# Accumulating transfers moved from one stage to another, and an order between GpSimd's additions and VectorE's two-operand operations

## The chip, the cores and the metric

The kernel runs on one core of one Trainium2 chip. The core has five engines that run side by side and wait for one another through semaphores: TensorE (PE in the profile: matmuls, with weight loads listed as PEld), VectorE (DVE), ScalarE (ACT), GpSimd (POOL) and SyncE (SP), which issues most of the DMA transfers. The metric is the device time of one execution in microseconds (us), the median of several runs. It was 2028.37 us before the change (three runs, 2027.73 to 2028.91).

## What is computed

Two layers of a decoder trunk on a sequence of 1024 tokens with 1024 channels, in float32. A layer has a mixer block (latent attention, a gated convolution, causal pooling, window attention, side by side) and a feed-forward block, each with a residual add:

```python
for l in range(DEPTH):
    h = rmsnorm(x, attn_norm[l])
    proj = h @ w_in[l]
    ...
    x = x + mixed @ w_o[l]
    h2 = rmsnorm(x, ffn_norm[l])
    gate, up = jnp.split(h2 @ w_gate_up[l], 2, axis=-1)
    x = x + (jax.nn.silu(gate) * up) @ w_down[l]
return rmsnorm(x, final_norm)
```

The feed-forward block has 2816 hidden channels, 22 tiles of 128.

## The kernel before

**Staging.** Activations are kept with channels on the 128 partitions and tokens along the free dimension, in two halves of 512 tokens. Each float32 matrix product is made of three matmuls: every operand is split into a high part in a rounded format (a cast on ScalarE, L368) and a low part (original minus high, a subtraction on VectorE, L371), and high x high, high x low and low x high are summed in PSUM (`mm3`, L348). So every weight tile passes through ScalarE and VectorE before TensorE can use it. The order of the stages, for each of the two layers, is: projections and mixers, output projection, gate/up (L1727 and after), down projection.

**Gate/up.** The gate/up and down products use a scheme with seven block products in place of eight, which needs sums of weight blocks. A step handles one f of the 22 hidden tiles: seven products of twelve matmuls (B11, B21, N2, N1, T3, B22, T4). Step 0 is done plainly. For steps 3 to 21 GpSimd makes the sums: three additions in `GateUp.sums` (L1330 to L1332) and one in `sum4` (L1360), each 128x512, for the step that follows. For steps 1 and 2 there is no time for that at the stage's start. Their sums lie ready in DRAM (`made`, buffers gd), built earlier by accumulating DMA transfers that GpSimd issues: a plain transfer writes a weight block into gd, and transfers with an add put further blocks on top. `gu_made(l)` (L306) is a generator that issues one of six such transfers for each of the two tiles at every call of `next`, twelve a layer. Each is held (`paced`, L297) until the matmul that was traced last before it has run, and one on the same bytes waits for the one before it. The sums are read at L1324, L1354 and L1365.

**Who calls the generator.** `project()` (L540) multiplies by one tile of the input weights for both halves; a layer has twelve such calls. Each begins with two calls of `next(sums, None)`, so a layer's twelve transfers go out during its own first six projections. `dn_made` yields nothing here, because `DN_MADE` is empty.

**GpSimd's other work.** In gate/up it also multiplies the SiLU by the norm factor (`silu`, L1570 on ScalarE, then L1572 on GpSimd; VectorE's L1564 takes the result) and makes sums of down weights in quarters (`dn_sum`, L1650, loaded by L1643, stored by L1653). In the mixers it clears parts of score tiles (L1158). On VectorE, L1450, L1776 and L1788 add PSUM results to copies, L449 multiplies, and `combos` (L1581, L1583) combines activations.

**The order of the work.** The program is traced, and then the class `Order` plans it: it simulates the five queues with a cost for each instruction, ranks instructions by when their results are due, improves the order with random trials, and picks the best of its plans by trials with drawn delays. The planned order of each queue is then imposed (`impose`): instructions of one queue follow one another as planned, without any semaphore. In this simulation a VectorE operation whose operands all lie in SBUF (kind "two": tensor by tensor, tensor by scalar, copy) and an addition on GpSimd (kind "pool") hold one port in turn: each waits for the other's end, less 0.14. `passing` gives the time that a transfer takes on the DMA engines, `costs` its time to landing, and `LATE` is added to loads.

Of the kernel before, what the change touches and what calls it, by code (L numbers as in the profile page):

```python
# [20 lines left out]
P = 128  # L21
D = 1024
S = 1024
L = 2
# [102 lines left out]
def trunk_kernel(ctx: ExitStack, tc: tile.TileContext, ins, out, given=None, ends=None):  # L127
# [212 lines left out]
    sums = iter(())  # L340
# [177 lines left out]
    for l in range(L):  # L518
        if l == 0:
            expect_layer(0)  # L520
        sums = chain(gu_made(l), dn_made(l))


        def proj(w, t, tag="mm"):
# [13 lines left out]
            return p  # L538

        def project():  # L540
            next(sums, None)
            next(sums, None)
            w = take()
            pp = [proj(w, t) for t in range(2)]
            ahead()
            return pp
# [399 lines left out]
        for t in range(2):  # L946
            s = F.half()
# [580 lines left out]


        acts = {f: [None, None] for f in range(3)}  # L1530

        def plain(u):

# [200 lines left out]
        for f in range(3, NFF):  # L1734
# [2 lines left out]
            wnn = GateUp(f + 2) if f + 2 < NFF else None  # L1737
            end = f == NFF - 1
            gu_start(w, lambda: pending and second(*pending))
            if f % 2:  # L1740
                g = f // 2
                sp.dma_start(ad_of(B11, g), F.ap(acts[2 * g][HALVES.index(0)]))
# [192 lines left out]
class Order:  # L1935
# [54 lines left out]

    @classmethod
    def passing(cls, i):
        return cls.size(i.outs[0]) * P * 4 / 400e3 if i.opcode == "DMACopy" else 0.0

    @classmethod
    def wide(cls, i):
# [17 lines left out]
    def costs(cls, i):  # L2014
# [5 lines left out]
        if op == "DMACopy":  # L2020
            t = cls.passing(i)
            if e == "Pool":
                return 1.5 * t + 3.5, 0.9
            if cls.kinds(i) == "load":
                return t + (1.85 if t < 0.7 else 2.1), 0.34
            return t + 1.35, 0.34
# [37 lines left out]
    def run(self, rank, back=False, fixed=None, draw=None):  # L2064
# [16 lines left out]
        order = {e: [] for e in self.ENGINES}  # L2081
        flying, served = deque(), 0.0
        port = {"two": 0.0, "pool": 0.0}
        other = {"two": "pool", "pool": "two"}
        for k in range(self.n):
            if not left[k]:
# [8 lines left out]
        while todo:  # L2095
# [34 lines left out]
            seen, taken = cost[k]  # L2130
            if draw:
                late = 2.5 * draw.random() if draw.random() < 0.25 else 0.0
                if e in ("DVE", "Activation", "Pool"):
                    more = draw.gauss(0.0, 0.02) * seen
                    seen, taken = seen + more, taken + more
            order[e].append(k)
            if back:
                free[e] = t + taken * (self.SHARED if kind[k] == "pool" else 1.0)
                end[k] = -free[e]
            else:  # L2140
                if kind[k] in port:
                    more = max(0.0, port[other[kind[k]]] - t - self.LEAST)
                    seen, taken = seen + more, taken + more
                    port[kind[k]] = t + seen
                free[e], end[k] = t + taken, t + seen
                if self.moved[k]:
                    if kind[k] == "load":
                        end[k] += late
                    served = end[k] = max(end[k], served + self.moved[k])
                if e == "SP":  # L2150
                    flying.append(end[k])
                    if len(flying) > self.LANES:
                        flying.popleft()
            for j, sync in ahead[k]:
# [9 lines left out]
                if not left[j] and fixed is None:  # L2164
                    heapq.heappush(later[self.engine[j]], (ready[j], j))
        return end, order

    def trial(self, order):

# [86 lines left out]
def scheduled_kernel(fresh, ins_of, rounds=1):  # L2256

    def trace(banks, ends, order=None):  # L2260
        nc = fresh()
        ins, out = ins_of(nc)
        with tile.TileContext(nc) as tc:
# [4 lines left out]
                if Order.queue(i) in Order.ENGINES and i.opcode != "TilePoolBoundary"  # L2268
            ]
            if order is not None:  # L2270
                Order.impose(tc, traced, order)
        return nc, traced, asked

    nc, traced, asked = trace(None, None)
# [1 line left out]
    for slow in SLOW:  # L2276
        plan, asked, first.slow = first, tried, slow
        end = plan.find()[2]
        for _ in range(rounds):
# [3 lines left out]
            best = plan.find()  # L2283
            end = best[2]
            order = plan.improve(best, 30)[1]
            found.append((plan.trial(order), given, order))
    best = min(found, key=lambda x: x[0])
    return trace(*best[1], best[2])[0]


def _constants():
# [132 lines left out]
```

## Time and profile before

| what | value |
|---|---|
| median of three runs | 2028.37 us |
| the profiled execution, its own time | 2028.42 us |
| its span, first to last instruction | 2026.6 us |
| granted TensorE clock, mean | 0.999 |
| DMA, share of 16 engines for SyncE's queue | 47.0% |
| DMA, share for GpSimd's queue | 3.3% |
| mean DMA rate | 167 GB/s |

The profile page starts with each engine's busy time. A row of a group reads: line of the kernel, engine, operation, tiles written and read, shape and count, then busy us and mean ns of one, then the idle time of that engine just ahead of these instructions and what ended it. Waits read: who waited, for whom, us in total, how often, the longest. A timeline row reads: start, length, engine, line, operation, and in brackets the idle time ahead of it and what released it. TensorE's matmuls overlap one another, and their ends are modelled, so its busy time says that it had work, not that it ran at full pitch. The stages can be told from the windows: in layer 0 mixers run to about 400 us, gate/up to about 800, the down projection to about 1000; layer 1 follows about 1003 us later.

### The profile page before, as it was taken

The page shows a single profiled execution, that of the slowest core. Times are in us where ns is not written, and L with a number is a line of the kernel's source. Part 1 is how long each engine was busy: PE and PEld are TensorE (multiplying, and loading weights), DVE is VectorE, ACT ScalarE, POOL GpSimd, SP SyncE. Part 2 cuts the span into 40 slices and gives each one's busy share as a digit, 9 for nine tenths or more (in the row PEclk, how much of TensorE's full clock was granted, in tenths as well). Part 3 has the DMA queues.
Part 4 walks back from the last instruction along what each step waited for, and adds up shares of the span by engine and source line. Part 5 has one row for each costly group of instructions (what it writes and reads, how often), then busy time and mean ns, then how long its engine had stood idle before and what let it go on. Part 6 is the DMA issues. An engine that isn't in the chain of part 4 may idle for free.

```text
span 2026.6 us, 26712 instructions
## 1 busy us (share of the span) xinstructions
PE 2015.0 (99%) x9418; PEld 1679.6 (83%) x9418; DVE 1521.4 (75%) x2330; ACT 1023.4 (50%) x1770; POOL 570.3 (28%) x428
## 2 busy tenths in 40 slices
PE   9999999999999999999999999999999999999998
PEld 8888888888888888888888888888888888888887
DVE  8789988997666668776646898789976766785554
ACT  8457657743333335555533676678333333354343
POOL 0100000057776772000001000000687677710000
PEclk9999999999999999999999999999999999999999
DMA  6531223345545547998835234242554554487552
GB/s 207 110 63 45 75 101 112 113 141 195 178 163 198 178 162 268 378 352 294 278 97 131 63 94 137 81 136 102 174 172 167 201 172 168 163 312 254 184 179 84
DMA packets 154231, 338.56 MB, mean 167 GB/s; under 512 B 14960, under 2 KB 62192, under 8 KB 154096
## 3 DMA queue, kind: packets, MB, share of 16 engines
q1 hardware_dynamic: 149616, 325.31, 47.0%
q0 software_dynamic: 4480, 11.54, 3.3%
q8 instruction: 74, 1.21, 0.3%
q14 instruction: 61, 0.50, 0.1%
HBM read 241.36 MB, written 105.91 MB: 171 GB/s over the span
## 4 chain that ended last, share of the span: by engine, by line
PE 98%; ACT 1%; DVE 0%; DMA 0%; issue 0%; DVEq 0%; ACTq 0%
PE ps_mm L348 38%; PE ps_s L348 30%; PE ps_t L348 12%; PE ps_pv L348 8%; PE ps_pv L1161 2%; PE ps_t L1149 2%; PE ps_s L1091 1%; PE ps_s L1092 1%; PE ps_s L1093 1%; PE ps_s L962 1%; PE ps_pv L763 1%; PE ps_s L685 1%; PE ps_t L428 1%; PE ps_t L751 1%; DMA u<-in_w_gu 0%; ACT u L368 0%
## 5 line engine op out<-in xcount | busy, mean ns | idle before, releaser
L348 PE MATMUL ps_mm<-u,u 128*128 128x512 f32 (+1 forms) x3378 | 825.4, 388 | 1.0 <-DVE tm L449 0.9
L348 PEld LDWEIGHTS ps_mm<-u,u 128*128 128x128 f32 x3378 | 616.8, 188 | 120.7 <-DVE tm L449 1.3
L371 DVE TENSOR_TENSOR u<-u,u 128x1024 fp32r<-128x1024 f32 (+3 forms) x461 | 508.7, 1124 | 182.0 <-ACT u L368 159.7
L348 PE MATMUL ps_s<-u,u 128*128 128x512 f32 x2670 | 634.1, 389 | 0.1
L348 PEld LDWEIGHTS ps_s<-u,u 128*128 128x128 f32 x2670 | 501.2, 188 | 104.7 <-DVE u L1298 0.5
L368 ACT CAST u<-u 128x1024 fp32r<-128x1024 f32 (+3 forms) x461 | 389.4, 864 | 376.4 <-DMA u<-ad 68.6
L348 PE MATMUL ps_t<-u,u 128*128 128x512 f32 (+1 forms) x1124 | 253.5, 377 | 0.1
L1572 POOL TENSOR_TENSOR tm<-tm,u 128x512 f32<-128x512 f32 x80 | 141.1, 1764 | 341.5 <-ACT tm L1570 335.7
L348 PEld LDWEIGHTS ps_t<-u,u 128*128 128x128 f32 x1124 | 202.5, 188 | 39.4 <-DVE u L1379 0.5
L348 PE MATMUL ps_pv<-u,u 128*128 128x512 f32 x744 | 177.4, 389 | 0.0
L348 PEld LDWEIGHTS ps_pv<-u,u 128*128 128x128 f32 x744 | 139.6, 188 | 29.0
L322 POOL DMA_DIRECT2D gd<-in_w_gu x24 | 21.3, 888 | 413.1 <-PE ps_t L348 280.7
L1158 POOL MEMSET u<- 128x128 f32 x32 | 5.9, 210 | 427.0 <-PE ps_mm L348 191.7
L1570 ACT ACTIVATE tm<-tm 128x512 f32<-128x512 f32 x80 | 50.6, 632 | 133.2 <-DVE tm L449 133.2
L1438 ACT COPY tm<-ps_s 128x512 f32<-128x512 f32 x61 | 35.8, 588 | 107.2 <-PE ps_s L348 107.1
L368 ACT CAST u<-ps_t 128x512 fp32r<-128x512 f32 (+3 forms) x132 | 64.3, 503 | 48.7 <-PE ps_t L1149 26.4
L371 DVE TENSOR_TENSOR u<-ps_t,u 128x512 fp32r<-128x512 f32 (+3 forms) x132 | 74.8, 582 | 16.0 <-ACT u L368 14.8
L1650 POOL TENSOR_TENSOR u<-u,u 128x352 f32<-128x352 f32 x64 | 80.0, 1251 | 1.4
L1360 POOL TENSOR_TENSOR u<-u 128x512 f32<-128x512 f32 x38 | 68.1, 1793 | 39.7 <-DVE u L371 39.7
L373 ACT ACTIVATE u<-u,par 128x512 fp32r<-128x512 f32 x99 | 69.7, 716 | 18.0 <-DVE u L1298 8.5
L412 ACT ACTIVATE tm<-u 128x512 f32<-128x512 f32 (+1 forms) x91 | 53.9, 599 | 47.2 <-DVE u L1841 39.6
L374 DVE SCALAR_TENSOR_TENSOR u<-u,par,u 128x512 fp32r<-128x512 f32 x99 | 72.3, 745 | 6.1 <-ACT u L373 5.6
(205 smaller groups left out, 2296.6 us busy)
## 6 DMA issues: line engine op xcount, KB each, us to landing
u<-in_w_gu SPq DMA_DIRECT2D x84, 512.0 KB, 4.1
ad<-u SPq DMA_DIRECT2D x154, 256.0 KB, 3.2
u<-ad SPq DMA_DIRECT2D x70, 512.0 KB, 5.8
u<-in_w_dn SPq DMA_DIRECT2D x64, 352.0 KB, 3.3
qd<-u SPq DMA_DIRECT2D x64, 352.0 KB, 2.6
u<-in_w_in SPq DMA_DIRECT2D x43, 512.0 KB, 4.8
u<-qd SPq DMA_DIRECT2D x32, 512.0 KB, 5.3
u<-in_w_dn SPq DMA_DIRECT2D x24, 512.0 KB, 5.4
```

The source lines that it names most:

```text
L348: last_mm = pe.matmul(o, w, r, start=start and k == 0 and i == 0, stop=stop and k == n - 1 and i == 2, skip_group_check=again,)
L368: a = act.copy(hi, f)
L371: dve.tensor_tensor(out=lo, in0=f, in1=rd(hi), op=ALU.subtract)
L373: a = act.activation(hi, f, AF.Copy, scale=gain)
L374: dve.scalar_tensor_tensor(out=lo, in0=f, scalar=gain, in1=rd(hi), op0=ALU.mult, op1=ALU.subtract)
L412: act.activation(q, f, AF.Square)
L1149: pe.transpose(p[:, b * P : (b + 1) * P], pr[b][j // 4][:, (j % 4) * P : (j % 4 + 1) * P], ident,)
L1161: pe.matmul(py[:, c0:], v_of(j, h), R.ap(s)[:, c0:], start=j == 0 and n == 0, stop=j == nj - 1 and n == 1,)
L1360: pool.tensor_tensor(out=q4, in0=q4, in1=F.ap(self.raw[1] + 1), op=ALU.add)
L1570: last_silu = act.activation(g, g, AF.Silu)
L1572: pool.tensor_tensor(out=g, in0=g, in1=r, op=ALU.mult)
L1650: pool.tensor_tensor(out=o, in0=a, in1=b, op=ALU.add)
```

## The change

The change has four parts.

1. Layer 1's twelve accumulating transfers leave layer 1's projections. A generator `made_next = gu_made(l + 1)` is made in layer 0, and each gate/up step from 3 on takes one transfer from it, just after `gu_start`. Layer 1's `project` finds nothing to issue.
2. Layer 0's transfers go one, not two, to a projection.
3. The planner's figures for GpSimd's transfers change: 2.5 times the passing time on the DMA engines, other constants to landing, loads twice as late while such a transfer is under way, and larger drawn delays then.
4. `Order.turns` walks through the planned order and pairs an addition on GpSimd with the last VectorE operation of kind "two" that ends before it starts, if one has ended since the pair before. `impose` adds a dependency with a semaphore for each pair: the addition then waits for that operation.

```diff
-        sums = chain(gu_made(l), dn_made(l))
+        sums = chain(gu_made(l) if l == 0 else (), dn_made(l))
...
         def project():
             next(sums, None)
-            next(sums, None)
             w = take()
...
         acts = {f: [None, None] for f in range(3)}
+        made_next = gu_made(l + 1) if l + 1 < L else iter(())
...
             gu_start(w, lambda: pending and second(*pending))
+            if l + 1 < L:
+                next(made_next, None)
             if f % 2:
...
     def passing(cls, i):
-        return cls.size(i.outs[0]) * P * 4 / 400e3 if i.opcode == "DMACopy" else 0.0
+        if i.opcode != "DMACopy":
+            return 0.0
+        t = cls.size(i.outs[0]) * P * 4 / 400e3
+        return t * (2.5 if cls.queue(i) == "Pool" else 1.0)
...
             if e == "Pool":
-                return 1.5 * t + 3.5, 0.9
+                return 1.2 * t + 3.0, 0.9
...
+        summed = 0.0
...
                 late = 2.5 * draw.random() if draw.random() < 0.25 else 0.0
+                if t < summed:
+                    late += 4.0 * draw.random() if draw.random() < 0.4 else 0.0
...
                     if kind[k] == "load":
                         end[k] += late
+                        if t < summed and not draw and fixed is None:
+                            end[k] += late
+                    elif e == "Pool":
+                        summed = end[k]
...
+    def turns(self, order):
+
+        end, _ = self.run(None, fixed=order)
+        start = [x - s for x, (s, _) in zip(end, self.cost)]
+        two = [k for k in order["DVE"] if self.kind[k] == "two"]
+        pairs, i = [], 0
+        for g in order["Pool"]:
+            if self.kind[g] != "pool":
+                continue
+            d = None
+            while i < len(two) and end[two[i]] <= start[g] + self.LEAST:
+                d = two[i]
+                i += 1
+            if d is not None:
+                pairs.append((d, g))
+        return pairs
...
-    def impose(tc, traced, order):
+    def impose(tc, traced, order, turns):
+        for a, b in turns:
+            tc.add_manual_dep(
+                traced[b],
+                traced[a].name,
+                mybir.DependencyInfo(mybir.DependencyClass.Sync, mybir.DependencyReason.DATA),
+                reason="turn",
+            )
```

The rest of the diff hands `turns` from the planner to `impose`.

More of the change, by code (lines that the diff above doesn't have):

```diff
@@ L2256, in scheduled_kernel, with trace @@
 def scheduled_kernel(fresh, ins_of, rounds=1):
-    def trace(banks, ends, order=None):
+    def trace(banks, ends, order=None, turns=()):
         nc = fresh()
@@ L2270, in trace @@
             if order is not None:
-                Order.impose(tc, traced, order)
+                Order.impose(tc, traced, order, turns)
         return nc, traced, asked
@@ L2285, in scheduled_kernel @@
             order = plan.improve(best, 30)[1]
-            found.append((plan.trial(order), given, order))
+            found.append((plan.trial(order), given, order, plan.turns(order)))
     best = min(found, key=lambda x: x[0])
-    return trace(*best[1], best[2])[0]
+    return trace(*best[1], *best[2:])[0]
 def _constants():
```

## The prediction

> **What bounds the kernel now.** I read the page first: the busy shares, then the chain that ended last, then the waits of TensorE (PE), and last the stages by windows.
>
> ```profile
> PE 2015.0 (99%) x9418; PEld 1679.6 (83%) x9418; DVE 1521.4 (75%) x2330; ACT 1023.4 (50%) x1770; POOL 570.3 (28%) x428
> PE 98%; ACT 1%; DVE 0%; DMA 0%; issue 0%; DVEq 0%; ACTq 0%
> PE ps_pv L579 <- DVE ones_r L198: 1.3, 1, 1.3
> PE ps_mm L348 <- DVE tm L449: 0.9, 1, 0.9
> PE ps_s L435 <- ACT tm L434: 0.5, 1, 0.5
> ```
>
> The second line is the chain by engine; the last three are all of TensorE's waits in the span: 2.7 us. Span minus busy time is 2026.6 - 2015.0 = 11.6 us, and most of it lies at the two ends, as the chain in order of time shows:
>
> ```profile
> 1.32 4.65 PE ps_pv L579 x20
> 93.21 21.79 PE ps_mm L348 x96
> 41.95 3.68 PE ps_mm L348 x16
> 2017.46 0.71 PE ps_s L435 x2
> ```
>
> The first matmul starts at 1.3 us and the last ends at 2018.2, so 8.4 us follow it; 11.6 - 1.3 - 8.4 leaves 1.9 us of visible idle time between. Busy time hides short bubbles, because the matmuls overlap, so I count matmuls by stage. Columns of the next view: stretch, its length, PE, PEld, DVE, ACT, POOL busy with counts, clock, DMA share, GB/s.
>
> ```profile
> 50.00:400.00 350.00, 349.02 (x1744) 292.38 (x1744) 309.31 (x648) 225.88 (x490) 13.28 (x27) 1.00 0.32 90
> 450.00:750.00 300.00, 300.00 (x1325) 248.39 (x1325) 204.73 (x209) 103.88 (x142) 223.01 (x158) 1.00 0.54 182
> 1050.00:1400.00 350.00, 349.93 (x1746) 292.64 (x1745) 289.95 (x624) 221.51 (x482) 12.75 (x27) 1.00 0.37 108
> 1450.00:1750.00 300.00, 300.00 (x1325) 248.43 (x1324) 209.44 (x211) 104.75 (x144) 220.61 (x156) 1.00 0.53 182
> ```
>
> In gate/up (rows 2 and 4) 300/1325 = 0.2264 us a matmul, the same number in both layers: full pitch, nothing to win there. In the mixers (rows 1 and 3) the chain's pieces run from 21.79/96 = 0.2270 to 3.68/16 = 0.2300 us, so bubbles hide between 0.0006 and 0.0036 us in each of 1744 + 1746 matmuls: an estimate of 2 to 13 us in all, in pieces far under 0.1 us. The granted clock is 1.00. So TensorE sets the time, and the change can shorten only what those bubbles and the 1.9 us hold.
>
> **The change part by part.**
>
> *Twelve transfers leave layer 1's projections; layer 0's twelve go one, not two, to a projection.* The accumulating transfers (L322) build the weight sums of gate/up steps 1 and 2 in DRAM.
>
> ```profile
> L322 POOL DMA_DIRECT2D gd<-in_w_gu x24: 551/846/1172, 40.9 to 1120.5; - x24
> L1324 SPq DMA_DIRECT2D u<-gd x4: 382/536/1466, 346.0 to 1351.8; - x4
>   POOL gd L322: 75.3, 13
>   ACT u L368: 5.5, 3
> DMA to landing us min/median/max: 3.1/5.3/10.5
> 117.02 0.85 POOL L322 DMA_DIRECT2D gd<-in_w_gu  x1 [6.90 <-DVE sm L694]
> gd<-in_w_gu POOLq DMA_DIRECT2D x20, 512.0 KB, 6.5
> 40.00:130.00 90.00, 90.00 (x458) 76.03 (x457) 71.47 (x168) 37.79 (x95) 10.69 (x12) 1.00 0.49 96
> u<-in_w_in SPq DMA_DIRECT2D x4, 512.0 KB, 3.5
> 213.98 0.35 POOL L1158 MEMSET u<- 128x128 f32 x2 [96.11 <-PE ps_mm L348]
> ```
>
> Rows three and four name all who waited for such a transfer or its result: the next of its kind on GpSimd, and ScalarE 5.5 us. TensorE is not among them. A weight load (in_w_in) lands after a median 3.5 us both in 40 to 125 us, where layer 0's twelve run, and in 125 to 230, where none does. So taking them out of layer 1 frees nothing TensorE waits for: 0 us. In layer 0 twelve projections now carry one each. The last was issued at 117 us; the twelfth projection is traced just ahead of the code that clears the first score tile, at 214, so I estimate the last issue near there. The sums are first read at 346: some 130 us stay, against a landing of at most 10.5. What it is moved past on GpSimd's queue is the clearing of score tiles (L1158), first at 214 us after 96 us of idle time: one issue (0.85 us) and at worst one landing ahead of it. 0 us.
>
> *The twelve go to layer 0's gate/up, one a step.* A step is seven products of twelve matmuls, 84 x 0.2264 = 19.0 us. GpSimd is busy 223.01/300 of it, 14.1 us, so 4.9 are idle. One issue of 0.85 us makes it 15.0 of 19.0. The predecessor it must wait for was issued 19 us earlier and lands in 10.5 at most, and its other wait, for a TensorE matmul just traced, is placed by the plan. Queued behind it are the sums for the next step (L1330 to L1332, L1360), the down-projection sums (L1650) and the product of the SiLU (L1572); for these wait ScalarE's split and VectorE's L1564. Cost 0 while the 4.9 us hold. On the DMA side each adds 512 KB to a stage at a share of 0.54, and the landings above show no queueing at 0.49 where they ran before: 0 us, at worst some tenths for a load that lands late.
>
> [...]
>
> *GpSimd's additions wait for VectorE's two-operand operations.* The plan pairs an addition with the last such operation that ends before it and adds a semaphore wait. Now the trace has both engines holding each other up:
>
> ```profile
> 397.23 1.30 POOL L1572 TENSOR_TENSOR tm<-tm,u 128x512 f32<-128x512 f32 x1 [63.37 <-ACT tm L1570]
> 415.26 6.83 POOL L1572 TENSOR_TENSOR tm<-tm,u 128x512 f32<-128x512 f32 x1 [16.73 <-ACT tm L1570]
> 415.56 4.16 DVE L371 TENSOR_TENSOR u<-u,u 128x512 fp32r<-128x512 f32 x5
> 811.61 1.21 DVE L371 TENSOR_TENSOR u<-u,u 128x1024 fp32r<-128x1024 f32 x1
> 589.70 0.69 DVE L449 TENSOR_TENSOR tm<-tm,u 128x512 f32<-128x512 f32 x1
> 589.80 1.39 POOL L1650 TENSOR_TENSOR u<-u,u 128x352 f32<-128x352 f32 x1
> 590.32 1.97 DVE L371 TENSOR_TENSOR u<-u,u 128x1024 fp32r<-128x1024 f32 x1
> ```
>
> An addition alone takes 1.30 us; behind an unbroken run of VectorE operations it took 6.83. VectorE's long split takes 1.21 us alone, 1.97 with an addition between. So they exclude each other, and the wait mostly renames time already lost. Where it isn't neutral is the last three rows: the addition was already standing at 589.80 when L449 ended at 590.39, and got in ahead of the split that was issued at 590.32. Told to wait for L449's end, it comes after the split: GpSimd loses one slot of 1.21 us, VectorE gains it.
>
> Is a slot covered? VectorE reaches TensorE's results ahead of time, which is the margin (450 to 750 us):
>
> ```profile
> POOL tm L1572 <- ACT tm L1570: 55.8, 20, 6.1
> POOL u L1360 <- DVE u L371: 17.1, 13, 2.7
> DVE tm L1788 <- PE ps_mm L348: 13.2, 7, 2.0
> DVE tm L1776 <- PE ps_s L348: 10.6, 6, 2.6
> DVE u L1564 <- POOL tm L1572: 7.1, 10, 1.2
> ```
>
> Its waits for products average 13.2/7 = 1.9 and 10.6/6 = 1.8 us, while TensorE waits for none. A delay of GpSimd that reaches VectorE through L1564 or a split uses up this margin first, and GpSimd's own waits for ScalarE (55.8 us) let it catch up within a step. One slot, 1.21 us, fits into 1.8; two in a row, 2.4, don't. Bounds: below, at best 2.7 us, all that TensorE ever waits; above, 0.6 us (2.4 - 1.8) in every one of 19 steps of two layers, 23 us. I take 0.2 us, near the lower rows, since TensorE's count per 300 us is identical in two layers whose VectorE and GpSimd times differ.
>
> *The plan is made anew.* Its figures for GpSimd's transfers, its lateness of loads and its random trials change, so every queue's order changes, in both layers. The mixers, where margins are thin, are the place: layers 0 and 1 are two such orders of the same work, 1744 and 1746 matmuls in 350 us, so they differ by 2 x 0.2264 = 0.5 us. I take 0, with 1 us either way for two stages.
>
> The sum, against the profiled execution of 2028.42 us (span 2026.6 and 1.8 around it; the median of the runs is 2028.37): 0 + 0 + 0 + 0.2 + 0 gives **2028.6 us**.
>
> **The rivals.**
>
> *Nothing is renamed at all* (0.24): GpSimd is idle before most groups of additions, the paired operation has ended when they come, and the time is 2028.4. The 55.8 us of waits for ScalarE speak for it, the 6.83 us row shows that collisions exist. Same verdict as the forecast.
>
> *GpSimd falls behind* (0.13, slower): the price is the lost slot, and it decides from two slots in a row, 2.4 us against 1.8. For it: VectorE's run of five splits without letting GpSimd in; a wait that ends only when such a run has begun. Against it: 4.9 us idle in each step. At one step in three of 38 it gives 13 x 0.6 = 8 us, 2036; at all of them 2051.
>
> *The moved issue is held* (0.03, slower): a GpSimd instruction was once held 6.83 - 1.30 = 5.5 us. If each of the twelve issues were, it would exceed the idle 4.9 by 0.6: 12 x 0.6 = 7 us, 2036. [...]
>
> *The new order is tighter* (0.04): the 1.9 us of idle time go and a fifth of 13 us of bubbles: 2024.1. No row ties those bubbles to GpSimd or its transfers.
>
> **How the numbers follow.** The forecast has 0.56. A measurement of this kernel can tell about 0.2%, 4.1 us, from no change. Within it are the forecast, the first rival and a quarter of the tighter order: 0.56 + 0.24 + 0.01 = 0.81. Slower by more: 0.13 + 0.03 = 0.16. Faster by more: 0.03. The range goes down by the 1.9 us of idle time, to 2026.5, and up to 2033.0, half the way to the 2036 of the slower rivals; outside lie most of these and the tighter order, under 0.2.
>
> **What would show it.**
>
> ```profile
> L1572 POOL TENSOR_TENSOR tm<-tm,u 128x512 f32<-128x512 f32 x80 | 141.1, 1764 | 341.5 <-ACT tm L1570 335.7
> ```
>
> Right: 1325 matmuls again in 300 us of gate/up in both layers, twelve L322 issues of about 0.85 us between some 430 and 700 us and none after 1050, shorter additions on GpSimd (L1572's mean under its 1764 ns) with more waits on VectorE ahead of them, and the same few TensorE waits. Wrong: TensorE waits on VectorE or ScalarE in gate/up that repeat each 19 us (a lost slot), L322 issues of several us (held issues), a ScalarE split waiting for a late gd load, or mixers whose matmul count in 350 us moves by over 10.

## The result and the profile after

The changed kernel takes 2032.45 us (median of 20 runs, 2031.4 to 2039.52), the kernel before, run beside it, 2028.34 us (20 runs, 2027.73 to 2029.64). The ratio is 1.0024 with a 95% interval of 1.0018 to 1.0031: slower, by about 4 us. The profiled execution took 2031.92 us, with a span of 2029.8.

The page's busy shares of the changed kernel, one row of part 1:

```profile
PE 2015.9 (99%) x9418; PEld 1678.2 (83%) x9418; DVE 1512.5 (75%) x2330; ACT 1022.3 (50%) x1770; POOL 535.3 (26%) x428
```

GpSimd's 570.3 us have become 535.3: fewer collisions with VectorE, as the change intends. TensorE's busy time rose by 0.9 us and the span by 3.2, so new idle time has come up. TensorE's four longest waits in the changed kernel (who waited, for whom, us in total, times, longest):

```profile
PE ps_t L348 <- DVE u L1564: 1.4, 1, 1.4
PE ps_pv L578 <- DVE ones_r L198: 1.3, 1, 1.3
PE ps_s L1090 <- ACT u L1109: 1.1, 1, 1.1
PE ps_s L435 <- ACT tm L434: 0.5, 1, 0.5
```

The first is new. The 1.1 us, in layer 0's mixers from 231.0 us on, stand about where the kernel before had 0.9 us on L449, from 227.1. (The lines of the three sums, L1330 to L1332 before, are L1329 to L1331 now; L1360 is L1359, L1776 and L1788 are L1778 and L1790.) The stages of the changed kernel, with the columns as before:

```profile
50.00:400.00 350.00, 348.46 (x1740) 290.93 (x1740) 308.20 (x648) 226.34 (x489) 14.38 (x28) 1.00 0.32 90
450.00:750.00 300.00, 298.40 (x1313) 245.87 (x1312) 209.17 (x208) 104.18 (x143) 223.79 (x167) 1.00 0.66 199
1050.00:1400.00 350.00, 349.88 (x1751) 293.03 (x1750) 289.65 (x624) 219.90 (x481) 2.86 (x16) 1.00 0.29 93
1450.00:1750.00 300.00, 300.00 (x1325) 248.43 (x1324) 200.08 (x213) 104.42 (x143) 207.20 (x156) 1.00 0.53 181
```

Layer 0's gate/up, which now carries the transfers, has 1313 matmuls where it had 1325: 12 x 0.2264 = 2.7 us. Layer 1's gate/up, with the waits but without transfers, is at 1325 still. Layer 0's mixers went from 1744 to 1740, 0.9 us, and layer 1's from 1746 to 1751.

Counts are coarse, so for the comparisons below each matmul's distance to the next was taken from the traces, less the median distance of its kind before, and summed by stretch. That is TensorE's lost time, up to a constant of the stretch. Columns: kernel, stretches in us, the profiled execution's own time.

```
                          50-400  450-750  1050-1400  1400-1450  1750-end   own time
before                      5.13    -0.44       4.79      -0.07      1.18    2028.42
after                       6.16     2.23       4.16       0.06      1.64    2031.92
e3  waits only              5.15    -0.13       4.35       0.76      1.68    2030.30
e4  waits, nothing moved    5.08    -0.12       4.49       0.76      1.69    2029.36
e9  one a projection        7.05    -0.44       6.94       0.81      1.17    2033.17
e1  after, no waits         6.29    -0.44       4.06       0.05      1.10    2028.74
e13 the same again          6.58     8.13       4.39       0.19      1.10    2038.22
e17 no waits, other order   6.03     3.50       4.82       0.01      1.42    2033.50
e12 L0's sums small         5.90     2.30       5.38       0.07      1.11    2032.33
e5  gate/up's sums small    6.25    -0.44       4.94       0.05      1.10    2029.41
e10 moved, two a proj.      5.09    -0.39       4.77      -0.07      1.17    2028.26
e15 e10 with waits          5.09     1.27       4.64       0.92      1.72    2030.86
```

In after against before, 1.0 us is lost in layer 0's mixers, 2.7 in its gate/up and 0.5 at the end, and 0.6 is won in layer 1's mixers. The last is within the scatter: e1, e5, e12 and e13, which run the changed kernel's order, have 4.1 to 5.4 there. Every stretch has a suspect: the order, the moved transfers, the waits.

Two rows of the page show the waits at work, GpSimd's product and VectorE's operation that takes it:

```profile
L1572 POOL TENSOR_TENSOR tm<-tm,u 128x512 f32<-128x512 f32 x80 | 129.8, 1623 | 301.6 <-ACT tm L1570 185.7
...
L1564 DVE SCALAR_TENSOR_TENSOR u<-tm 128x512 f32<-128x512 f32 x38 | 39.6, 1043 | 47.8 <-POOL tm L1572 47.8
```

The second of them in the kernel before:

```profile
L1564 DVE SCALAR_TENSOR_TENSOR u<-tm 128x512 f32<-128x512 f32 x38 | 41.2, 1085 | 12.2 <-POOL tm L1572 12.2
```

A product is 141 ns shorter than before on average (1764), but VectorE now stands 47.8 us waiting for products, where it stood 12.2. The view of the moved line, durations in ns as minimum/median/maximum, then first and last start:

```profile
L322 POOL DMA_DIRECT2D gd<-in_w_gu x24: 559/855/1194, 40.5 to 657.9; - x24
```

No issue was held. The one large stall of TensorE in gate/up begins at 653.1 us. The timeline of the changed kernel ahead of it (start, length, engine, line; idle time and releaser in brackets):

```profile
639.43 1.14 POOL L322 DMA_DIRECT2D gd<-in_w_gu  x1
...
641.20 3.57 DVE L371 TENSOR_TENSOR u<-u,u 128x1024 fp32r<-128x1024 f32 x1 [0.64 <-ACT u L368]
...
648.82 0.62 ACT L368 CAST u<-u 128x512 fp32r<-128x512 f32 x1 [6.02 <-DMA u<-in_w_gu]
...
649.47 0.69 DVE L371 TENSOR_TENSOR u<-u,u 128x512 fp32r<-128x512 f32 x1 [3.78 <-ACT u L368]
...
650.24 1.29 POOL L1330 TENSOR_TENSOR u<-u,u 128x512 f32<-128x512 f32 x1 [1.95 <-DVE u L371]
```

A transfer goes out; VectorE's split behind it takes 3.57 us in place of 1.21; ScalarE's cast then stands 6.0 us for a DMA; VectorE's split waits for that cast 3.78, and GpSimd's addition, by its new wait, for that split 1.95. All three engines are late together, and TensorE waits 1.4 us for L1564.

The bracket of the cast names a load (in_w_gu), but by the trace the two loads about there were issued at 638.2 and 644.9 and landed 4.1 and 5.0 us later, one before the cast's wait began, the other after it had ended. What landed as the cast started, at 648.8, is a store of down-weight sums. Its issue, and the time to landing of all such stores in 450 to 700 us:

```profile
641.58 0.37 SPq L1653 DMA_DIRECT2D qd<-u  x1
...
DMA to landing us min/median/max: 2.3/2.5/7.2
```

It is the slowest, 7.2 us; in layer 1's gate/up none takes over 4.1. So the cast very likely stood for this store, issued 2.15 us behind the transfer.

Loads are late beside the transfers too. Two answers for the loads of down weights in the changed kernel, first in layer 0's gate/up, with the transfers beside them, then in layer 1's, without; the second row of each is the time to landing in us:

```profile
L1643 SPq DMA_DIRECT2D u<-in_w_dn x26: 372/384/512, 461.1 to 698.3; - x26
...
DMA to landing us min/median/max: 3.0/3.6/8.9
...
L1643 SPq DMA_DIRECT2D u<-in_w_dn x26: 378/383/500, 1464.6 to 1699.9; - x26
...
DMA to landing us min/median/max: 3.0/3.2/3.9
```

Without transfers the slowest load lands after 3.9 us, with them after 8.9.

### The profile page after: what moved, and what is told of

Read it like the earlier page. It is cut to its first block, busy times and chain, and to the rows that moved or that the text cites. A ratio compares the mean times of both kernels' runs of the same rounds, so it can differ in the third digit from the quotient of the medians.

```text
span 2029.8 us, 26797 instructions
## 1 busy us (share of the span) xinstructions
PE 2015.9 (99%) x9418; PEld 1678.2 (83%) x9418; DVE 1512.5 (75%) x2330; ACT 1022.3 (50%) x1770; POOL 535.3 (26%) x428
## 3 DMA queue, kind: packets, MB, share of 16 engines
q8 instruction: 74, 1.21, 0.2%
## 5 line engine op out<-in xcount | busy, mean ns | idle before, releaser
L371 DVE TENSOR_TENSOR u<-u,u 128x1024 fp32r<-128x1024 f32 (+3 forms) x461 | 497.3, 1100 | 201.0 <-ACT u L368 162.1
L1572 POOL TENSOR_TENSOR tm<-tm,u 128x512 f32<-128x512 f32 x80 | 129.8, 1623 | 301.6 <-ACT tm L1570 185.7
L1564 DVE SCALAR_TENSOR_TENSOR u<-tm 128x512 f32<-128x512 f32 x38 | 39.6, 1043 | 47.8 <-POOL tm L1572 47.8
L1650 POOL TENSOR_TENSOR u<-u 128x352 f32<-128x352 f32 x64 | 70.0, 1097 | 16.3 <-DVE tm L1778 5.2
```

Of the source, the lines that this page charges most:

```text
L371: dve.tensor_tensor(out=lo, in0=f, in1=rd(hi), op=ALU.subtract)
L1564: dve.scalar_tensor_tensor(out=o, in0=a, scalar=-1.0, in1=b, op0=ALU.mult, op1=ALU.mult)
L1572: pool.tensor_tensor(out=g, in0=g, in1=r, op=ALU.mult)
L1650: pool.tensor_tensor(out=o, in0=a, in1=b, op=ALU.add)
```

## The experiments

Theories at the start: **the waits** cost what is lost (they put GpSimd a slot late), **the transfers** do, in the stage that they were moved to, or **the order**, made anew, does. All runs are five rounds against the kernel before on the same chip; times are medians, "+" is against that kernel's median, and the bracket after a ratio is its 95% interval.

### First set: which part

e1, the changed kernel without the waits, in its own order:

```diff
-            found.append((plan.trial(order), given, order, plan.turns(order)))
+            found.append((plan.trial(order), given, order, ()))
```

> The changed kernel with its planned order in every queue, but no addition on GpSimd waits for VectorE. Contention theory (the moved transfers delay other transfers on the DMA engines of layer 0's gate/up, and ScalarE and VectorE wait behind a late one): still slow, 2031.5 to 2033. Lost-slot theory (an addition told to wait comes one VectorE operation later): back to 2028.0 to 2029.0. New-order theory (the plan is simply worse): 2031.5 to 2033.

e2, the changed kernel with the eight adding transfers in gate/up cut to an eighth of their columns:

```diff
...
-                paced(pool.dma_start(d, a, **more))
+                paced(pool.dma_start(*(cut(d, a) if l and more else (d, a)), **more))
...
```

The lines left out define `cut` and let the planner still count the whole size.

> The changed kernel with its order and its waits, but the eight accumulating transfers of the twelve that were moved to layer 0's gate/up carry an eighth of their columns, so layer 1's sums for steps 1 and 2 are incomplete. GpSimd still issues every one. Contention theory: most of the loss goes, 2028.5 to 2030, and no store or load in that stage takes 7 us. Lost-slot and new-order theories: unchanged, 2031.5 to 2033.

e3, the kernel before in its own order, with `turns` and `impose` of the changed kernel added, nothing else:

> The kernel before with its planned order, its transfers where they were, and the waits of GpSimd's additions for VectorE added. Contention and new-order theories: 2028.0 to 2029.0, within 0.05% of the kernel before. Lost-slot theory: 2031 to 2033.

e4, the changed kernel with all transfers where they were, the waits and the planner's new figures kept:

```diff
-        sums = chain(gu_made(l) if l == 0 else (), dn_made(l))
+        sums = chain(gu_made(l), dn_made(l))
...
             next(sums, None)
+            next(sums, None)
...
-        made_next = gu_made(l + 1) if l + 1 < L else iter(())
...
-            if l + 1 < L:
-                next(made_next, None)
```

> The changed kernel with all transfers back in each layer's own projections, two to a projection; the planner's new figures and the waits stay, and the order is planned anew. Contention theory: 2028.0 to 2029.0. Lost-slot theory: 2031 to 2033. New-order theory: no number follows from it, anything from 2028 to 2033.

Measured, with the kernel before at 2028.15 us: e1 2031.02 (2028.74 to 2037.9), ratio 1.0018 (1.0009 to 1.0027); e2 2030.29, 1.0011 (1.0002 to 1.0020); e3 2030.61, 1.0011 (1.0002 to 1.0020); e4 2030.02, 1.0009 (1.0001 to 1.0018). Every part alone costs something: the waits +2.5 us in the order of before (e3, whose fastest run, 2029.75, is behind the slowest of the kernel before, 2029.63) and +1.9 with the planner's new figures (e4); the rest without waits +2.9 (e1), with a spread of 9 us from run to run. e4's order is all but that of before (on VectorE two neighbours of 2330 operations are exchanged), so the new figures alone remake little of it. e1's profiled execution was its fastest and shows no loss in gate/up (-0.44 in the table), so its cause had to wait for e13.

How e3 loses shows best at the start of layer 1's gate/up, where VectorE has little lead yet. The kernel before, three rows of its timeline:

```profile
1437.37 3.54 DVE L371 TENSOR_TENSOR u<-u,u 128x1024 fp32r<-128x1024 f32 x2
...
1439.79 2.27 POOL L1360 TENSOR_TENSOR u<-u 128x512 f32<-128x512 f32 x1
...
1440.84 0.68 DVE L1564 SCALAR_TENSOR_TENSOR u<-ps_s,u 128x512 f32<-128x512 f32 x1
```

e3, the same three instructions:

```profile
1438.18 4.18 DVE L371 TENSOR_TENSOR u<-u,u 128x1024 fp32r<-128x1024 f32 x2
...
1442.51 1.27 POOL L1360 TENSOR_TENSOR u<-u 128x512 f32<-128x512 f32 x1 [1.23 <-DVE u L371]
...
1442.28 0.68 DVE L1564 SCALAR_TENSOR_TENSOR u<-ps_s,u 128x512 f32<-128x512 f32 x1
```

Before, the addition L1360 had started while the splits ran, and ended at 1442.06. In e3 it stands 1.23 us until the splits are over, and ends at 1443.78. The splits gained nothing: with GpSimd one addition behind, others fall on them, and they take 4.18 us in place of 3.54. L1564 comes 1.44 us later than before; by 0.4 of that e3's TensorE was behind already, the rest is lost here. It is what TensorE waits for, in e3's answer for 1430 to 1446 us:

```profile
PE ps_s L348 <- DVE u L1564: 0.6, 1, 0.6
```

Compared one by one with the same additions before, over stretches of the gate/up stages, e3's end 0.8 to 1.3 us later on average, and up to 4.5 us, with TensorE's own lag taken off. Its window of 450 to 750 us and GpSimd's first two waits in it:

```profile
450.00:750.00 300.00, 299.99 (x1324) 248.16 (x1323) 198.01 (x209) 104.28 (x143) 205.42 (x156) 1.00 0.54 181
```

```profile
POOL tm L1572 <- ACT tm L1570: 27.6, 6, 4.6
POOL tm L1572 <- DVE u L371: 21.7, 11, 5.7
```

GpSimd's busy time fell from 223.01 to 205.42, so 17.6 us of collisions are gone; but its waits for VectorE in this stage rose from the 17.1 us of before to 51.5 in sum, of which the second row is the largest part.

### Second set: do the pieces add up

Compared place by place by line, tiles and shape, the traces of the changed kernel, e1, e2, e5, e6, e12, e13 and e16 have the same order on every engine. So these differ in the named part alone.

e5 is e2 without the waits:

> The changed kernel's order without the waits of GpSimd's additions, and with the eight accumulating transfers in layer 0's gate/up cut to an eighth of their columns (layer 1's sums for steps 1 and 2 are incomplete). If the loss is the waits plus the contention and nothing else, both gone: 2028.0 to 2029.0, with a spread under 2 us. If the new order itself is worse: 2030 or more.

e6 is the changed kernel once more, on this chip:

> The changed kernel once more, beside the others of this set. Both-causes theory: 2031.5 to 2033, the sum of the two parts (about 2 us for the waits, about 2 for the transfers), and again single executions of 2034 and more.

e7 and e8 split e3's waits in two: e7 keeps the 80 whose VectorE operation is followed at once by another two-operand one, e8 the other 57.

```diff
-            if d is not None:
+            at = {a: b for a, b in zip(order["DVE"], order["DVE"][1:])}
+            if d is not None and self.kind[at.get(d, d)] == "two":
```

> The kernel before with only those waits whose VectorE operation is followed directly, in VectorE's queue, by another two-operand operation: 80 additions more that wait for VectorE. Lost-slot theory: these carry the cost, 2029.8 to 2030.8. If every wait costs the same by its number, 2029.5 and about equal to the other half.

> The kernel before with only those waits whose VectorE operation is followed by one that reads PSUM or by none of the kind: 57 additions more that wait for VectorE. Lost-slot theory: nearly free, 2028.0 to 2028.8. If every wait costs the same by its number, 2029.1.

Measured, with the kernel before at 2028.04: e5 2028.99, 1.0005 (0.9996 to 1.0014); e6 2035.27 (6 runs, 2032.34 to 2037.93), 1.0034 (1.0022 to 1.0045); e7 2029.17, 1.0003 (0.9994 to 1.0012); e8 2028.79, 1.0003 (0.9994 to 1.0012). e7 and e8 cost +1.1 and +0.75, 1.9 in sum, like e3's 2.5 within the error: 0.014 us a wait in e7 (1.13/80) and 0.013 in e8 (0.75/57). Nothing here points at the tight waits alone; but an interval is 1.8 us either way, and those of e5, e7 and e8 include no change. e2 less e5 is the waits again, in the changed order: (+2.1) - (+0.95) = 1.2 us. e1 less e5, both without waits and planned with the cost of whole transfers, is the size of the moved transfers: (+2.9) - (+0.95) = 1.9 us. e6 came out above the 2031.5 to 2033 expected; it varies by 5.6 us between its own runs, and its profiled execution (2036.7 us) has stalls all over, in the mixers too.

### Third set: the projections, and the move without the waits

e9 is the kernel before with one transfer a projection in layer 0, planned with the old figures. e10 is the changed kernel without waits and with two a projection in layer 0 (`next(sums, None)` twice, as before), so the move to gate/up alone. e11 is e3 with each wait put on the two-operand operation before the paired one.

```diff
             next(sums, None)
-            next(sums, None)
+            next(sums if l else iter(()), None)
```

> The kernel before with layer 0's twelve transfers one, not two, to a projection; layer 1 keeps its two to a projection, and the order is planned anew with the old figures. If spreading them over all twelve projections sets one beside a weight load that TensorE needs at once (about 165 to 185 us): 2028.5 to 2029.3, with a TensorE wait behind a ScalarE split there. As the prediction had it: 2028.0 to 2028.4.

> The changed kernel without the waits of GpSimd's additions and with layer 0's transfers two to a projection again; layer 1's stay in layer 0's gate/up, and the order is planned anew. What is left is the contention in gate/up: about 2 us, 2029.5 to 2031, with single executions well above. If the contention comes from the projections alone: 2028.0 to 2028.6.

```diff
-                pairs.append((d, g))
+                pairs.append((two[max(i - 2, 0)], g))
```

> The kernel before with each paired addition waiting for the two-operand operation of VectorE before the paired one: 100 additions more that wait for VectorE, mostly for one already done. If a wait costs by being there: 0.013 us each, 1.3 us, 2029.4. If it costs by holding GpSimd until the last moment: 2028.0 to 2028.6.

Measured, with the kernel before at 2028.32: e9 2033.07, 1.0022 (1.0013 to 1.0031); e10 2028.26, 0.9998 (0.9989 to 1.0007); e11 2028.17, 0.9997 (0.9989 to 1.0006).

e9 surprises: +4.8 us for spreading transfers out. The table puts it into the mixers of both layers (7.05 and 6.94), though layer 1's transfers are where they were. So in layer 1 it is the order that the planner found, not what the transfers meet; in layer 0 this run can't tell the two apart. e10 says that the moved transfers are free in some order: its row of gate/up is full again.

```profile
450.00:750.00 300.00, 300.00 (x1325) 248.38 (x1325) 217.60 (x211) 104.52 (x142) 236.17 (x168) 1.00 0.66 200
```

e11 says that a wait costs nothing by being there. It costs where it holds an addition until the last operation that is planned to end before it, since then any lateness of VectorE becomes lateness of GpSimd.

### Fourth set: repeats, and the transfers by stage

e12 is the order of e5 with the sizes swapped: layer 0's adding transfers cut to an eighth, those in gate/up whole, no waits. e13 repeats e1, e14 repeats e10, and e15 is e10 with the waits.

```diff
...
-                paced(pool.dma_start(*(cut(d, a) if l and more else (d, a)), **more))
+                paced(pool.dma_start(*(cut(d, a) if more and not l else (d, a)), **more))
...
```

> The changed kernel's order without the waits of GpSimd's additions; the accumulating transfers of layer 0, one to a projection, carry an eighth of their columns (layer 0's sums for steps 1 and 2 are incomplete), those in gate/up are whole. If the loss sits with the transfers in gate/up: as the same kernel with whole transfers, about 2031, with a spread of several us. If it sits with layer 0's transfers beside the projections: 2028.5 to 2029.3 and a narrow spread.

> The changed kernel without the waits of GpSimd's additions, once more, beside the others of this set: 2030 to 2032, with single executions over 2033, as both readings have it. Its profile is wanted too, since the first one was the fastest of eleven executions.

> No waits, layer 0's transfers two to a projection, layer 1's in layer 0's gate/up, once more beside the others of this set. If the move to gate/up is free: 2028.0 to 2028.6, the kernel before. If the first result was luck of the chip: 2030 to 2031.

> The same with the waits of GpSimd's additions: the changed kernel but for layer 0's transfers, two to a projection. If the waits cost about 2 us and the move nothing: 2030 to 2031. If the waits leave no room for the transfers in gate/up, so that the two together cost more than each: 2031.5 or more.

Measured, with the kernel before at 2027.95: e12 2031.51, 1.0019 (1.0010 to 1.0028); e13 2031.65 (2028.58 to 2038.22), 1.0021 (1.0013 to 1.0029); e14 2028.14, 1.0001 (0.9993 to 1.0010); e15 2030.88, 1.0019 (1.0010 to 1.0027). Both repeats agree with their first runs (e13 +3.7, e1 +2.9). e15 less e14 is the waits in a third order: 2.7 us (e15's fastest run took 2030.11, e14's slowest 2028.72). By the table 1.7 of it is lost in layer 0's gate/up, beside the transfers, so it isn't the waits by themselves. e12 puts the loss of the transfers into gate/up (+3.6 with layer 0's small), and layer 0's mixers stay at 5.90 there: so the bytes of layer 0's transfers aren't what costs 0.8 us more than before there.

e13's profiled execution was its slowest, and shows how gate/up loses without waits. Its timeline, VectorE's row first and then GpSimd's:

```profile
644.18 8.14 DVE L371 TENSOR_TENSOR u<-u,u 128x1024 fp32r<-128x1024 f32 x1 [0.64 <-ACT u L368]
...
642.41 1.14 POOL L322 DMA_DIRECT2D gd<-in_w_gu  x1
643.17 1.36 POOL L1650 TENSOR_TENSOR u<-u,u 128x352 f32<-128x352 f32 x1
644.32 1.44 POOL L1572 TENSOR_TENSOR tm<-tm,u 128x512 f32<-128x512 f32 x1
645.58 1.08 POOL L1650 TENSOR_TENSOR u<-u,u 128x352 f32<-128x352 f32 x1
646.47 1.42 POOL L1359 TENSOR_TENSOR u<-u 128x512 f32<-128x512 f32 x1
647.72 1.07 POOL L1650 TENSOR_TENSOR u<-u 128x352 f32<-128x352 f32 x1
648.62 1.40 POOL L1329 TENSOR_TENSOR u<-u,u 128x512 f32<-128x512 f32 x1
649.87 1.37 POOL L1330 TENSOR_TENSOR u<-u,u 128x512 f32<-128x512 f32 x1
651.31 2.14 POOL L1331 TENSOR_TENSOR u<-u,u 128x512 f32<-128x512 f32 x1
```

One split of VectorE, 1.21 us when alone, lasts 8.14 us, while GpSimd runs seven additions behind the issue without a gap. Each begins before the record of the one ahead has ended, by 0.2 us (643.17 + 1.36 = 644.53 against 644.32); elsewhere additions that follow each other overlap by 0.07 us at most. The run ends at L1331, which waits for the addition just ahead and starts 0.08 us after its end; then VectorE gets in, and L1331 takes 2.14 us. The runs at 526 us in e12, e13 and e17 end at L1331 too. In the kernel before and in every run with the transfers in the projections, no two-operand operation of VectorE after 380 us took over 2.36 us; in every traced execution with the moved transfers some did, and each overlap of over 0.1 us lies in such a run behind an issue. How long the longest lasts goes with the loss, as long as there are no waits: with one of 7.6 us or more (e12, e13, e17) gate/up lost 2.7 to 8.6 us against before, with 2.9 to 4.9 (e1, e5, e10, e14) at most 0.1. The changed kernel, with the waits, has none over 3.71 and lost 2.7 all the same. In e13 TensorE then waited for VectorE's L1778:

```profile
PE ps_s L348 <- DVE tm L1778: 3.4, 1, 3.4
PE ps_pv L348 <- DVE tm L1778: 1.8, 1, 1.8
```

The second of these begins at 533.2 us, behind a split of 7.59 us at 526.7. And the stall costs more than its length. e13's windows around it:

```profile
649.00:653.00 4.00, 0.57 (x4) 0.15 (x2) 4.00 (x3) 0.62 (x1) 3.92 (x3) 0.88 0.72 271
653.00:656.00 3.00, 3.00 (x7) 2.42 (x8) 2.90 (x4) 0.57 (x1) 0.45 (x1) 0.50 0.43 109
656.00:659.00 3.00, 3.00 (x9) 2.28 (x8) 0.49 (x1) 0.98 (x2) 1.28 (x1) 0.53 0.26 99
659.00:662.00 3.00, 3.00 (x15) 2.44 (x14) 3.00 (x5) 0.62 (x3) 0.00 (x0) 1.00 0.28 107
```

The granted clock (third figure from the right) was 0.50 after the idle stretch, by the trace's record of it from 652.0 to 658.8 us. Rows two and three have 7 + 9 matmuls in place of the 15 of row four, at 1.00: (30 - 16) x 0.2264 = 3.2 us more.

### Fifth set: is it the shut-out, and is it the order

e16 is the changed kernel with waits only for additions among the first eight behind an issue, which should break up the long runs at little cost. e17 is e1 with other random numbers in the planner, e18 the kernel before with other random numbers.

```diff
...
+            after = 0 if self.moved[g] else after + 1
...
-            if d is not None:
+            if d is not None and after <= 8:
```

```diff
-        draw = random.Random(1)
+        draw = random.Random(2)
```

> The changed kernel in its own order, but only those of its waits whose addition is among the first eight behind a transfer of GpSimd's queue; the additions elsewhere wait for nothing new. Theory A (two causes: every wait costs a little, and in this order the transfers moved to gate/up let GpSimd shut VectorE out for several us): most of the cost of the waits goes, the worst shut-outs of 7.6 to 8.1 us go as well, so a time of 2029.0 to 2030.3 with little spread, and no two-operand operation of VectorE over 4.5 us in gate/up. Rival (the loss of this order without waits is not from shut-outs behind an issue): 2031 to 2032 with executions up to 2038, as in the runs of this order with no waits at all.

> The changed kernel without waits, and with other random numbers in the search that makes the order: same transfers at the same steps, another order. If what the transfers cost in gate/up hangs on the order that the search happens to find: anything from 2028 to 2032, and the profile shows fewer or more stalls of TensorE in 430 to 700 us than the 2031.0 and 2031.7 of the first order came with; within 0.5 us of 2031.3 speaks for a cost of the transfers whatever the order.

> The kernel before with other random numbers in the search, nothing else: what a mere change of order is worth. If orders differ by several us without any change of the work (as the one-a-projection order, 4.8 us slower, suggests): a time off 2028.2 by more than 1 us on either side, the difference in the mixers. If orders of one program are alike: 2027.8 to 2028.7.

Measured, with the kernel before at 2028.28: e16 2033.48 (2031.27 to 2035.0), 1.0023 (1.0014 to 1.0031); e17 2033.50 (7 runs, 2033.05 to 2038.0), 1.0027 (1.0016 to 1.0037); e18 2029.31, 1.0003 (0.9994 to 1.0012).

e16 was half a miss. The shut-outs went as expected, to 3.0 and 3.6 us, but the time is 3 us above the 2029.0 to 2030.3 that should have followed, and above that of the changed kernel's order without any waits. So the shut-outs can't be the whole loss of this order. Its profiled execution (2031.66 us, one of its fastest) has the stall of the changed kernel at the same place; its waits from 636 to 656 us:

```profile
ACT u L368 <- DMA qd<-u: 6.3, 1, 6.3
...
POOL u L1330 <- DVE u L371: 1.8, 1, 1.8
...
PE ps_t L348 <- DVE u L1564: 1.7, 1, 1.7
```

So where the waits cap the shut-out, by this trace a cast that stands 6 us for a store beside the transfer, with GpSimd's addition chained to VectorE behind it, gives the next stall. What made its other runs 2 us slower still than the profiled one is not seen.

e17, above every time expected for it, has the shut-out again in another order. Its timeline and, after it, two of its windows:

```profile
526.31 7.64 DVE L371 TENSOR_TENSOR u<-u,u 128x1024 fp32r<-128x1024 f32 x1 [0.29 <-ACT u L368]
```

```profile
535.00:538.00 3.00, 3.00 (x11) 2.40 (x10) 2.52 (x4) 0.63 (x1) 0.32 (x2) 0.68 0.41 120
538.00:541.00 3.00, 3.00 (x11) 2.35 (x11) 2.12 (x3) 0.00 (x0) 1.04 (x1) 0.75 0.87 333
```

Both windows are means: by the trace's record the clock was 0.50 from 536.1 to 539.5 us and 1.00 around that. So the loss in gate/up is no accident of one order, though e10's order is free of it. e18, nothing but another order, costs +1.0, with the loss in layer 1's mixers: that is about the size of an accident, though e18's interval includes no change.

## Why the prediction failed

The forecast was 2028.6, no change; it came out 3.9 us higher, inside the range. That it lies inside is luck: the upper end, 2033.0, is called half the way to 2036, but from 2028.6 that is 2032.3, and the rivals that it was taken from are not what happened. None of the prediction's signs of being wrong came (no issue was held, the mixers' counts moved by 4 and 5): for gate/up they looked for a loss that repeats each step, and what came was single stalls, seen in the count alone (1313 in place of 1325). Step by step:

**Twelve transfers leave layer 1's projections: 0.** Right. Layer 1's mixers lost 4.2 without them in the changed kernel and 4.5 to 4.8 in e10 and e14, against 4.8 before.

**Layer 0's go one a projection: 0.** Right for the transfers themselves (the last issue came at 202.0 us, all landed within 8.3, and e12's small ones leave the loss where it is), wrong for the stage. With one a projection its mixers lost 0.4 to 1.9 us more than before in the profiled executions of three orders (the changed kernel's, e17's, e9's; e6 with its stalls left out), with two a projection at most 0.2 more, in three orders also (that of before and all but the same in e4, e10's, e18's). Whether the place of the issues does this or the orders that the planner finds for it wasn't told apart.

**Twelve go to gate/up: 0, "at worst some tenths for a load that lands late".** Mis-sized, by about 2 us, in this order: e1 less e5 1.9, the changed kernel less e2 4.1 - 2.1 = 2.0. The idle time of GpSimd was there and no issue was held, as forecast; the cover failed because 4.9 us a step is a sum. Two ways of losing it were seen. Without the waits, GpSimd works off what has queued up behind an issue in one run that keeps VectorE out, for up to 8.14 us against VectorE's margin of 1.8. With the waits, as in the changed kernel itself, the longest is 3.71 us, and the stall comes from a store that lands late beside a transfer (7.2 us, median 2.5) and holds up cast, split and addition in turn. How much of the 2 us each makes in the median isn't shown. On the DMA side the landings beside layer 0's projections were the wrong rows to go by: in gate/up a down load landed after up to 8.9 us, not 3.9. The rival "the moved issue is held" looked for the opposite case, a GpSimd transfer that is held up. Here the transfers' issues stayed at 1.19 us at most, and VectorE was starved by what GpSimd ran behind them: in e13 the split of 8.14 us (1.21 alone) stood behind seven additions in a row and lost to each of them.

**The waits: 0.2.** Mis-sized tenfold: 2.5 and 1.9 us in the order of before (e3, e4), 1.2 in the changed one (e2 less e5) and 2.7 in that of e10, about 2. The mechanism was named in the rival (GpSimd a slot late, through L1564), but two assumptions failed. "The wait mostly renames time already lost" holds only for the collision that it removes; the addition then ends about a microsecond later and falls on other operations. And the margin of 1.8 us was a mean over a stage: e3's loss is at the start of gate/up and at its end (0.76 and 1.68 in the table, before -0.07 and 1.18), where VectorE has no such lead. The count that the 0.2 leaned on couldn't see this: in 300 us of gate/up e3 has 1324 matmuls in both layers, one less than before.

**The order made anew: 0, with 1 us either way.** e5, with neither waits nor whole transfers in gate/up, is at +0.95, most of it the loss in layer 0's mixers; e18 at +1.0. That is the edge of the bound, neither is clear of no change, and e9 with +4.8 shows that it was too narrow: two layers in one order were taken for two orders, and are two stages of one search.

In the changed order the parts are 0.95 for order and rest (e5), 1.2 for the waits (e2 less e5) and 2.0 for the moved transfers (the changed kernel less e2). That these give the 4.1 measured is so by construction; what it can be tested by is e1, which gives nearly the same prices the other way round (1.9 for the transfers, 4.1 - 2.9 = 1.2 for the waits). By its repeat e13 the waits are only 0.4, and e16, with a part of the waits, cost +5.2: prices of single parts are rough here. The rival that came nearest was "GpSimd falls behind", at a quarter of its price. Settled are that the waits cost about 2 us in an unchanged order (e3, and e4 near it) and that the move alone is free in one order (e10, e14). Open remains what makes e10's order free of the stalls, though the transfers in gate/up land as late there (after up to 10.1 us in e14, 10.0 in the changed kernel) and VectorE's worst splits last 4.1 us, and why runs of one program with moved transfers differ by up to 10 us (e13). No version was faster than the kernel before; e10, e11 and e14 equal it.

## What to carry to other kernels

Idle time of an engine that shuts another one out, as GpSimd did VectorE here, was no cover where its work came without gaps (seven additions in a row, a split of 8.14 us against a mean lead of 1.8): look at how long a run the engine makes behind a held instruction, and compare it with the smallest lead of the engine it shuts out, not with the mean. A wait that held an addition until the last moment that the plan foresaw turned lateness of VectorE into lateness of GpSimd (e3, +2.5 us); the same wait one operation earlier was free (e11, 2028.17 us beside 2028.32). Where an order is searched at random, run the old program in a second order first: here that moved the median by 1.0 us, a quarter of what was to be explained, though its interval includes no change.

## What the runs showed of the hardware

- Beside an unbroken run of seven GpSimd additions behind a DMA issue a two-operand operation of VectorE lasted 8.14 us (e13; 1.21 alone); the reverse, one addition behind VectorE's run, was 6.83 us before the change (1.30 alone).
- A stall of TensorE of 3.4 us (e13) came with 6.8 us at a granted clock of 0.50 (from 652.0 us, where the stall lasted until 653.0), one of 2.0 us (e17) with 3.4 us of it (from 536.1), while one of 2.4 us (e12) was followed by 1.00, in e12's windows behind it:

```profile
535.00:538.00 3.00, 3.00 (x15) 2.43 (x14) 2.82 (x5) 0.63 (x1) 0.32 (x2) 1.00 0.39 112
538.00:541.00 3.00, 3.00 (x15) 2.49 (x14) 3.00 (x4) 0.55 (x2) 1.09 (x1) 1.00 0.93 356
```

  So the length of the stall alone did not decide it in these three; what does was not shown. By the count of the windows above, the half rate cost 3.2 us in e13's slowest execution, of 9.6 between its fastest and its slowest. It is one source of the spread between runs.
- With accumulating transfers beside them, loads of 352 KB landed after up to 8.9 us in place of 3.9, and stores of 352 KB after up to 7.2 in place of 4.1 (the changed kernel, layer 0's gate/up against layer 1's). In layer 0's gate/up before the change, without such transfers, it was up to 4.2 for the loads and up to 5.9 for the stores.
